# Seven-product strips: another product order, low halves last, weights traced behind the copies

## The chip, the cores and the metric

The kernel runs on one core of one Trainium2 chip. The metric is the device time in microseconds, from launch to end, as the median of a few runs. Engines are named as the profile names them: PE (TensorE matmul; PEld is its weight load, which overlaps the matmuls), DVE (VectorE), ACT (ScalarE), POOL (GpSimd) and SP (SyncE, which issues most DMAs).

## The reference

Two residual layers on a 512 x 1024 input: layer 0 mixes tokens with gated linear attention, layer 1 with softmax attention, and each is followed by a gated MLP. The change touches the MLP alone, which runs once in each layer:

```
def conv_ffn(h, w_up, w_conv, b_conv, w_down):      # h: rmsnorm(x), 512 x 1024
    u = h @ w_up                                    # 512 x 5632
    u = depthwise conv of width 3 along the tokens (u) + b_conv
    val, gate = jnp.split(u, 2, axis=-1)            # 2816 each
    return (jax.nn.silu(gate) * val) @ w_down       # 512 x 1024
x = x + conv_ffn(rmsnorm(x, norm_ffn[i]), ...)
```

All inputs and outputs are float32.

## The kernel before, in words

Every float32 product is made of three matmuls on rounded halves: a tile is split into a high half (an ACT copy to float32r) and a low half (what is left, by DVE or by an adding DMA), and high x high, high x low and low x high are summed in PSUM. Weights go the same way: a raw piece of 128 x 1024 is loaded by SP (`W.load`), ACT writes its high half `wh` (line 319 or 271) and DVE its low half `wl` (line 320), or ACT writes minus the high half (line 272) and POOL issues a DMA that adds the raw weights to it (line 308). `W.flush` issues such waiting DMAs; `W.todo` lists the pieces in the order in which they are made, and `W.ahead(n)` makes the next n.

The MLP is worked in 22 chunks of 128 gate and 128 value features, m = 0 to 21 (`ffn`, `act_up`). Chunks 0 to 5, 9, 14 and 17 are plain (`plain_up`): two feature tiles of 24 matmuls of 512 columns. The other 13 (the list `SEVEN`) are done as 2 x 2 blocks with seven products in place of eight (`seven_up`), and so are two thirds of the down projection (`down_part`, two parts of four strips, called behind chunks 9 and 17). That makes 26 + 16 such strips in both layers. Each strip is seven calls of `product`; each product is four pairs of blocks x three matmuls of 256 columns, all of them line 1074 in the profile, where the result is called `r`. So a strip is 84 matmuls.

The seven products are numbered 1 to 7. Product 1 goes to a bank of its own and ACT copies it twice (`twice`, line 1129) into the bank `both`, whose halves are r1 and r2. Product 6 adds to r2, and ACT copies r2 to the first half of a bank r3 (line 1095 in `seven_up`, 1204 in `down_part`). Product 7 goes to r4 and is copied twice to a tile `u` (or `f`). Product 4 adds to r3's first half. Product 5 adds to r2, and ACT copies r2 to r3's second half (line 1102 or 1211). `add_seven` (line 1132, DVE) adds r3 to the tile: this is one of the two results of the strip, and `act_up` then works on it (line 1117 on ACT, 1118 and 1119 on DVE). Products 2 and 3 finish the other result in `both`. Product 1 of the next strip (`begin_up`, or `begin` in `down_part`) is put between 5 and 2, to give the copies time.

The weights of a strip are four pieces (`PLACE`): piece 0 serves products 1 and 4, piece 1 serves 6 and 2, piece 2 serves 7 and 5, piece 3 serves 3. `product` asks for a piece with `W.piece`, which also makes further pieces until `PAW` = 6 (or `PA` = 4) are waiting, all of that ahead of the product's own matmuls in the traced order. PSUM has eight banks: three for `acc` (both, plain results), two for `s` (r3), two for `pt` (products 1 and 7), one other. The tiles u, f and g share three buffers.

The order of the instructions on an engine follows the order in which they are traced, but the planner that lays them out passes over an instruction that is not ready by its own estimate and takes the next that is; `tc.issue_after` pins one behind another. On the chip each engine keeps the order that was laid out.

`rescale`, called in chunk 0, scales the input and splits it by `low_dma` into `nh` and `nl`; its four adding DMAs wait in `W.pending` until the next flush. `prepare_input` later works in place on the same scaled tiles.

Of the kernel before, what the change touches and what calls it, by code (L numbers as in the profile page):

```python
# [62 lines left out]
NQ, NPART = 4, 2  # L63
# [3 lines left out]
DOWN_AFTER = {9: 0, 17: 1}  # L67


SEVEN = (6, 7, 8, 10, 11, 12, 13, 15, 16, 18, 19, 20, 21)  # L70
UPA = 3
PA = 4
# [16 lines left out]
PAW = 6  # L89
# [11 lines left out]
def hybrid_encoder_kernel(  # L101
# [23 lines left out]
    pe, act, dve, pool, sync = nc.tensor, nc.scalar, nc.vector, nc.gpsimd, nc.sync  # L125
    mm = pe.matmul
# [8 lines left out]
    def nm(s):  # L135
        uid[0] += 1
        return f"{s}{uid[0]}"
# [3 lines left out]
    def bank(tag, n):  # L141
        return pp.tile([P, S], F32, tag=tag, bufs=PS[tag], name=nm(n))
# [33 lines left out]
    class Weights:  # L176
# [127 lines left out]
        def flush(self):  # L304

            for lo, r in self.pending:
                same = lo.dtype == F32R and r.dtype != F32R
                pool.dma_start(lo.bitcast(F32) if same else lo, r, accum_op=ALU.add)
            self.pending = []

        def split(self, hi, lo, r, pieces=1, first=False):
# [28 lines left out]
    W = Weights()  # L340
# [3 lines left out]
    def add_up(layer, chunks):  # L344
        for m in chunks:
            W.add(up[layer], (m,), 4 if m in SEVEN else 2)
            if m in SEVEN and m - 1 not in SEVEN and m - 1 not in DOWN_AFTER:
                W.todo[-5:-3] = W.todo[-4], W.todo[-5]

    def add_ffn(layer):  # L350
        first = 0
        for m, part in DOWN_AFTER.items():
            add_up(layer, range(first, m + 1))
            W.add(down_w[layer], range(part * NQ, (part + 1) * NQ), 4)
            at = len(W.todo) - 4 * NQ - 1
            W.todo[at : at + 2] = W.todo[at + 1], W.todo[at]
            first = m + 1
        add_up(layer, range(first, FC))
        W.add(down_w[layer], range(NPART * NQ, down_w[layer].shape[0]))
# [135 lines left out]
    def feature_tile(*a):  # L495
        for last in feature_steps(*a):
            pass
        return last
# [518 lines left out]
    def ffn(layer, norm, cw, nxt):  # L1017
# [5 lines left out]
        down = []  # L1023
# [4 lines left out]

        def rescale():

            for p in range(KC // 2):
                xr = big(F32, "xr")
                for i in range(2):
                    c = 2 * p + i
                    dve.scalar_tensor_tensor(xr[:, i * S : (i + 1) * S], x[c], norm.weight(c), norm.R, ALU.mult, ALU.mult)
                hi, lo = big(F32R, "nh"), big(F32R, "nl")
                W.low_dma(hi, lo, xr)
                scaled.append(xr)
                fresh.extend((hi[:, i * S : (i + 1) * S], lo[:, i * S : (i + 1) * S]) for i in range(2))

        def plain_up(m):

            pss = []
            for t in range(2):
                ps = bank("s" if t else "acc", "up")
                feature_tile(*W.half(up[layer], 2 * m + t, max(UPAW if W.wide else UPA, ahead.get((m, t), 1))), norm.hl if m < SWITCH else fresh, ps)
                pss.append(ps)
                if t == 0 and m not in DOWN_AFTER:
                    begin_up(m + 1)
                if t == 0 and m in DOWN_AFTER:  # L1050
                    down.append(down_part(DOWN_AFTER[m], m))
                    next(down[-1])
# [12 lines left out]
        def product(pieces, src, strip, pairs, i, dst, start):  # L1065
            h, o = PLACE[i]
            if h not in pieces:
                pieces[h] = W.piece(src, strip, h, PAW if W.wide else PA)
            wh, wl = pieces[h]
            for j, p in enumerate(pairs):  # L1070
                sl = slice(o + j * P, o + (j + 1) * P)
                mh, ml = p[i]
                for a, (w, m) in enumerate(((wh, mh), (wh, ml), (wl, mh))):
                    mm(dst, w[:, sl], m, start=start and j == 0 and a == 0, stop=j == len(pairs) - 1 and a == 2,  # L1074
                       skip_group_check=True)
            W.flush()

        def begin_up(m):
            if m in SEVEN:
                begun.append(seven_up(m))  # L1080
                next(begun[-1])

        def seven_up(m):

            pieces = {}
            go = lambda *a: product(pieces, up[layer], m, inputs, *a)
            r = bank("pt", "r1")[:, :H]
            go(1, r, True)
            both = bank("acc", "r")
            r1, r2 = both[:, :H], both[:, H:]  # L1090
            twice(both, r)
            yield
            go(6, r2, False)
            r3 = bank("s", "r3")
            act.activation(r3[:, :H], r2, AF.Copy)  # L1095
            r4 = bank("pt", "r4")[:, :H]
            go(7, r4, True)
            d = tmp("u", "u")
            twice(d, r4)
            go(4, r3[:, :H], False)  # L1100
            go(5, r2, False)
            act.activation(r3[:, H:], r2, AF.Copy)  # L1102
            add_seven(d, r3, r4)
            yield 1, d
            begin_up(m + 1)
            go(2, r1, False)
            go(3, r2, False)
            yield 0, both

# [15 lines left out]
        H = S // 2  # L1125

        def twice(d, r4):
            two = lambda a: a.rearrange("p (o t) -> p o t", t=H)
            act.activation(two(d), two(r4).to_broadcast([P, 2, H]), AF.Copy)

        def add_seven(d, r3, r4):
            dve.tensor_tensor(d, d, r3, ALU.add)
# [49 lines left out]
        def down_part(part, m):  # L1182

            pairs = [quads.pop(part * NQ + i) for i in range(NQ)]
            st = {}
            pieces = [{} for _ in range(NQ)]
            go = lambda n, *a: product(pieces[n], w_dn, part * NQ + n, pairs, *a)

            def begin(n):
                r = bank("pt", "r1")[:, :H]
                go(n, 1, r, True)
                st[n] = bank("acc", "r")
                twice(st[n], r)

            begin(0)
            yield
            for n in range(NQ):
                r, c, d = st[n], x_home[n][:, :S], x_home[n][:, S:]  # L1200
                r1, r2 = r[:, :H], r[:, H:]
                go(n, 6, r2, False)
                r3 = bank("s", "r3")
                act.activation(r3[:, :H], r2, AF.Copy)
                r4 = bank("pt", "r4")[:, :H]
                go(n, 7, r4, True)
                g, f = tmp("u", "g"), tmp("u", "f")
                twice(f, r4)
                go(n, 4, r3[:, :H], False)
                go(n, 5, r2, False)  # L1210
                act.activation(r3[:, H:], r2, AF.Copy)  # L1211
                add_seven(f, r3, r4)
                W.pending.append((d, f))
                if n + 1 < NQ:
                    begin(n + 1)
                else:
                    begin_up(m + 1)
                go(n, 2, r1, False)
                go(n, 3, r2, False)
                act.activation(g, r, AF.Copy)  # L1220
                W.pending.append((c, g))

        def end(c, ps):
# [13 lines left out]
        for m in range(FC):  # L1237
# [15 lines left out]
            else:  # L1253
                for i, y in enumerate(held):
                    t = big(F32R, "gu")
# [343 lines left out]
```

## Time and profile before

| | |
|---|---|
| median of 3 runs | 1087.01 us (1086.85 to 1087.84) |
| profiled execution, first to last instruction | 1085.5 us |
| PE busy | 1077.5 us (99%) |
| PEld busy | 966.4 us (89%) |
| DVE busy | 888.5 us (82%) |
| ACT busy | 721.1 us (66%) |
| POOL busy | 136.7 us (13%) |
| granted TensorE clock | 1.000 |

The table is of one execution; its device time is not given apart from its span, so the 1.5 us between the span and the median of the runs stand for what lies around the span. Busy time is the share in which an engine worked on an instruction at all; weight loads and matmuls of PE overlap, and matmuls are pipelined, so the duration of one is longer than the distance between two.

### The profile page before, as it was taken

Reading aid. Unit: us, or ns where it says so; the run is one execution under the profiler, and the core shown is the slowest. Engines: PE = TensorE matmul, PEld = TensorE weight load, DVE = VectorE, ACT = ScalarE, POOL = GpSimd, SP = SyncE. Lnnn points to the kernel's source line nnn. Section 1 sums busy time; section 2 is a strip of 40 time slices with the busy share of each in tenths; the row PEclk is TensorE's granted clock in tenths of the full one; section 3 lists DMA queues with packets and bytes.
Section 4 is the critical chain, followed back from the end, with each engine's and each line's share of the span. In section 5 each row is a group of like instructions: output and inputs, shape, how many; then the busy total and the mean of one; then the engine's idle time right before and its main releaser. Section 6 shows DMA issues by size and latency. Waiting matters only on the chain.

```text
span 1085.5 us, 17391 instructions
## 1 busy us (share of the span) xinstructions
PE 1077.5 (99%) x6672; PEld 966.4 (89%) x6672; DVE 888.5 (82%) x1327; ACT 721.1 (66%) x1134; POOL 136.7 (13%) x153
## 2 busy tenths in 40 slices
PE   9999999999999999999999999999999999999998
PEld 8888988888999999999988888888889999999997
DVE  7998967569898899988755588666989889998882
ACT  8679575478775676666574677656877567666660
POOL 0212112021001100010015333002110010001000
PEclk9999999999999999999999999999999999999999
DMA  8744446499545633274767475549863473227542
GB/s 301 187 126 106 122 141 215 154 207 204 127 125 127 145 120 111 77 177 121 252 149 162 127 204 164 164 158 202 206 148 124 105 166 116 100 80 157 136 175 78
DMA packets 55763, 164.52 MB, mean 152 GB/s; under 512 B 6528, under 2 KB 7040, under 8 KB 55680
## 3 DMA queue, kind: packets, MB, share of 16 engines
q1 hardware_dynamic: 36192, 112.66, 32.2%
q0 software_dynamic: 14592, 42.21, 21.7%
q10 hardware_dynamic: 4896, 8.55, 2.1%
q8 instruction: 52, 0.85, 0.3%
q14 instruction: 31, 0.25, 0.1%
HBM read 114.89 MB, written 14.68 MB: 119 GB/s over the span
## 4 chain that ended last, share of the span: by engine, by line
PE 87%; DVE 6%; ACT 3%; DMA 2%; issue 2%; POOL 0%; SPq 0%; DVEq 0%; ACTq 0%; POOLq 0%
PE r L1074 37%; PE op L535 8%; PE vg L652 7%; PE up L482 4%; PE up L483 4%; PE up L484 4%; PE dn L483 2%; PE dn L484 2%; PE dn L482 2%; PE av L509 1%; PE A L482 1%; DVE wl L320 1%; PE A L484 1%; DMA nl<-xr 1%; PE B L484 1%
## 5 line engine op out<-in xcount | busy, mean ns | idle before, releaser
L320 DVE TENSOR_TENSOR wl<-raw,wh 128x1024 fp32r<-128x1024 f32 x156 | 189.8, 1220 | 31.3 <-ACT wh L319 31.1
L319 ACT ACTIVATE wh<-raw 128x1024 fp32r<-128x1024 f32 x156 | 162.6, 1053 | 73.4 <-PE op L535 20.7
L1074 PE MATMUL r<-gu,wh 128*128 128x256 f32 x896 | 161.2, 282 | 0.0
L1074 PE MATMUL r<-xt,wh 128*128 128x256 f32 x832 | 151.1, 283 | 0.4 <-ACT r L1095 0.3
L1074 PEld LDWEIGHTS r<-gu,wh 128*128 128x128 f32 x896 | 139.3, 190 | 1.0 <-ACT r L1211 0.2
L1074 PEld LDWEIGHTS r<-xt,wh 128*128 128x128 f32 x832 | 129.2, 190 | 1.6 <-ACT r L1095 1.1
L1074 PE MATMUL r<-gu,wl 128*128 128x256 f32 x448 | 126.3, 283 | 0.0
L1074 PE MATMUL r<-xt,wl 128*128 128x256 f32 x416 | 117.2, 283 | 0.0
L1074 PE MATMUL r<-nh,wh 128*128 128x256 f32 x312 | 88.8, 285 | 0.3 <-ACT r L1102 0.3
L1074 PE MATMUL r<-nh,wl 128*128 128x256 f32 x312 | 88.2, 283 | 0.0
L1074 PE MATMUL r<-nl,wh 128*128 128x256 f32 x312 | 87.9, 282 | 0.0
L1074 PEld LDWEIGHTS r<-gu,wl 128*128 128x128 f32 x448 | 85.1, 190 | 0.0
L1074 PEld LDWEIGHTS r<-xt,wl 128*128 128x128 f32 x416 | 79.1, 190 | 0.0
L482 PE MATMUL up<-nh,wh 128*128 128x512 f32 x192 | 75.3, 392 | 0.0
L483 PE MATMUL up<-nl,wh 128*128 128x512 f32 x192 | 75.2, 392 | 0.0
L484 PE MATMUL up<-nh,wl 128*128 128x512 f32 x192 | 75.2, 392 | 0.0
L535 PE MATMUL op<-oT,wh 128*128 128x512 f32 x256 | 72.4, 393 | 0.0
L271 ACT ACTIVATE wh<-raw 128x1024 fp32r<-128x1024 f32 x36 | 38.0, 1056 | 38.2 <-PE up L483 11.5
L1074 PEld LDWEIGHTS r<-nh,wh 128*128 128x128 f32 x312 | 59.3, 190 | 2.9 <-ACT r L1102 2.6
L1074 PEld LDWEIGHTS r<-nl,wh 128*128 128x128 f32 x312 | 59.4, 190 | 0.2
L1074 PEld LDWEIGHTS r<-nh,wl 128*128 128x128 f32 x312 | 59.4, 190 | 0.0
L535 PEld LDWEIGHTS op<-oT,wh 128*128 128x128 f32 x256 | 47.4, 188 | 9.7 <-ACT oT L937 0.3
(299 smaller groups left out, 2761.6 us busy)
## 6 DMA issues: line engine op xcount, KB each, us to landing
raw<-in_w_up_dram SPq DMA_DIRECT2D x84, 512.0 KB, 4.6
raw<-in_w_down_dram SPq DMA_DIRECT2D x44, 512.0 KB, 3.7
wl<-raw POOLq DMA_DIRECT2D x20, 512.0 KB, 5.3
wl<-in_w_up_dram POOLq DMA_DIRECT2D x16, 512.0 KB, 7.8
ring<-p ACTq DMA_DIRECT2D x32, 256.0 KB, 2.6
xw<-in_xw_dram SPq DMA_DIRECT2D x8, 512.0 KB, 6.6
raw<-in_w_v_dram SPq DMA_DIRECT2D x8, 512.0 KB, 5.9
raw<-in_w_g_dram SPq DMA_DIRECT2D x8, 512.0 KB, 4.0
```

The costliest lines, as they stand in the source:

```text
L271: act.activation(hi, r, AF.Copy)
L319: act.activation(hi[:, sl], a, AF.Copy)
L320: dve.tensor_tensor(lo[:, sl], a, hi[:, sl].bitcast(F32), ALU.subtract)
L482: mm(ps, wh, mh, start=start, stop=False)
L483: mm(ps, wh, ml, start=False, stop=False)
L484: return mm(ps, wl, mh, start=False, stop=stop)
L509: mm(ps[j][:, :width], hl[k][i == 2][:, j * P : (j + 1) * P], (wl if i == 1 else wh)[:, sl], start=k == 0 and i == 0, stop=k == KC - 1 and ...
L535: mm(pss[ng][n], wt[:, sl], mv, start=k == late[0][0] and i == 0, stop=k == late[-1][-1] and i == 2)
L652: last = mm(ps[j], m[:, js], w[:, sl], start=i in (1, 7, 2) and p == 0 and a == 0, stop=i in (4, 2, 3) and p == 3 and a == 2, skip_group_c ...
L1074: mm(dst, w[:, sl], m, start=start and j == 0 and a == 0, stop=j == len(pairs) - 1 and a == 2, skip_group_check=True)
```

## The change

Five things are altered. Within a product, the eight matmuls with high halves of weights come first and the four with low halves last. `product` takes a function `then`, the ACT copy of its result, and traces it right behind the matmuls; only behind that are further weights made (`W.ahead`), and that now happens after each product. The order of the products of a strip becomes 1; 6, 7, 2, 5, [1 of the next], 4, 3, so that products 2 and 4 have changed places, and `add_seven` comes behind product 4 and so behind product 1 of the next strip. `rescale` flushes what is pending, and then issues each of its four adding DMAs as soon as it is traced, pinned behind the last weights' DMA. A swap in `W.todo` is made only where the chunk is not one of `SEVEN`; the two chunks to which the line applies, 9 and 17, are not, so the list stays what it was. `begin` gathers the two ways in which a next strip is begun.

```
-                pool.dma_start(lo.bitcast(F32) if same else lo, r, accum_op=ALU.add)
+                self.sent = pool.dma_start(lo.bitcast(F32) if same else lo, r, accum_op=ALU.add)
...
         def rescale():
+            W.flush()
+            sent = W.sent
             for p in range(KC // 2):
...
                 W.low_dma(hi, lo, xr)
+                with tc.issue_after(sent.ins):
+                    W.flush()
...
-        def product(pieces, src, strip, pairs, i, dst, start):
+        def product(pieces, src, strip, pairs, i, dst, start, then=None):
             h, o = PLACE[i]
             if h not in pieces:
-                pieces[h] = W.piece(src, strip, h, PAW if W.wide else PA)
+                pieces[h] = W.piece(src, strip, h, 0)
             wh, wl = pieces[h]
-            for j, p in enumerate(pairs):
-                sl = slice(o + j * P, o + (j + 1) * P)
-                mh, ml = p[i]
-                for a, (w, m) in enumerate(((wh, mh), (wh, ml), (wl, mh))):
-                    mm(dst, w[:, sl], m, ...)
+            steps = [(j, wh, a) for j in range(len(pairs)) for a in range(2)]
+            steps += [(j, wl, 0) for j in range(len(pairs))]
+            for n, (j, w, a) in enumerate(steps):
+                mm(dst, w[:, o + j * P : o + (j + 1) * P], pairs[j][i][a], ...)
+            if then is not None:
+                then()
+            W.ahead((PAW if W.wide else PA) - len(W.made))
             W.flush()
...
         def seven_up(m):
...
-            go(6, r2, False)
             r3 = bank("s", "r3")
-            act.activation(r3[:, :H], r2, AF.Copy)
+            go(6, r2, False, copy(r3[:, :H], r2))
             r4 = bank("pt", "r4")[:, :H]
-            go(7, r4, True)
             d = tmp("u", "u")
-            twice(d, r4)
+            go(7, r4, True, lambda: twice(d, r4))
+            go(2, r1, False)
+            go(5, r2, False, copy(r3[:, H:], r2))
+            begin(m)
             go(4, r3[:, :H], False)
-            go(5, r2, False)
-            act.activation(r3[:, H:], r2, AF.Copy)
             add_seven(d, r3, r4)
             yield 1, d
-            begin_up(m + 1)
-            go(2, r1, False)
             go(3, r2, False)
             yield 0, both
```

`down_part` is altered in the same way: 6, 7, 2, 5, [1 of the next], 4, `add_seven`, 3, with f's adding DMA behind product 4 and g's behind product 3.

More of the change, by code (lines that the diff above doesn't have):

```diff
@@ L355, in add_ffn @@
             at = len(W.todo) - 4 * NQ - 1
-            W.todo[at : at + 2] = W.todo[at + 1], W.todo[at]
+            if m not in SEVEN:
+                W.todo[at : at + 2] = W.todo[at + 1], W.todo[at]
             first = m + 1
@@ L1047, in plain_up @@
                 pss.append(ps)
-                if t == 0 and m not in DOWN_AFTER:
-                    begin_up(m + 1)
-                if t == 0 and m in DOWN_AFTER:
-                    down.append(down_part(DOWN_AFTER[m], m))
-                    next(down[-1])
+                if t == 0:
+                    begin(m)
                 if m == 0 and t == 0:
@@ L1081, in begin_up, with begin @@
                 next(begun[-1])
+        def begin(m):
+            if m in DOWN_AFTER:
+                down.append(down_part(DOWN_AFTER[m], m))
+                next(down[-1])
+            else:
+                begin_up(m + 1)
         def seven_up(m):
@@ L1086, in seven_up @@
             go = lambda *a: product(pieces, up[layer], m, inputs, *a)
-            r = bank("pt", "r1")[:, :H]
-            go(1, r, True)
-            both = bank("acc", "r")
+            copy = lambda o, i: lambda: act.activation(o, i, AF.Copy)
+            r, both = bank("pt", "r1")[:, :H], bank("acc", "r")
             r1, r2 = both[:, :H], both[:, H:]
-            twice(both, r)
+            go(1, r, True, lambda: twice(both, r))
             yield
-            go(6, r2, False)
             r3 = bank("s", "r3")
-            act.activation(r3[:, :H], r2, AF.Copy)
+            go(6, r2, False, copy(r3[:, :H], r2))
             r4 = bank("pt", "r4")[:, :H]
-            go(7, r4, True)
             d = tmp("u", "u")
-            twice(d, r4)
+            go(7, r4, True, lambda: twice(d, r4))
+            go(2, r1, False)
+            go(5, r2, False, copy(r3[:, H:], r2))
+            begin(m)
             go(4, r3[:, :H], False)
-            go(5, r2, False)
-            act.activation(r3[:, H:], r2, AF.Copy)
             add_seven(d, r3, r4)
             yield 1, d
-            begin_up(m + 1)
-            go(2, r1, False)
             go(3, r2, False)
@@ L1189, in down_part, with first @@
             go = lambda n, *a: product(pieces[n], w_dn, part * NQ + n, pairs, *a)
-            def begin(n):
+            copy = lambda o, i: lambda: act.activation(o, i, AF.Copy)
+            def first(n):
                 r = bank("pt", "r1")[:, :H]
-                go(n, 1, r, True)
                 st[n] = bank("acc", "r")
-                twice(st[n], r)
-            begin(0)
+                go(n, 1, r, True, lambda: twice(st[n], r))
+            first(0)
             yield
@@ L1201, in down_part @@
                 r1, r2 = r[:, :H], r[:, H:]
-                go(n, 6, r2, False)
                 r3 = bank("s", "r3")
-                act.activation(r3[:, :H], r2, AF.Copy)
+                go(n, 6, r2, False, copy(r3[:, :H], r2))
                 r4 = bank("pt", "r4")[:, :H]
-                go(n, 7, r4, True)
                 g, f = tmp("u", "g"), tmp("u", "f")
-                twice(f, r4)
+                go(n, 7, r4, True, lambda: twice(f, r4))
+                go(n, 2, r1, False)
+                go(n, 5, r2, False, copy(r3[:, H:], r2))
+                if n + 1 < NQ:
+                    first(n + 1)
+                else:
+                    begin_up(m + 1)
                 go(n, 4, r3[:, :H], False)
-                go(n, 5, r2, False)
-                act.activation(r3[:, H:], r2, AF.Copy)
                 add_seven(f, r3, r4)
                 W.pending.append((d, f))
[L1214 to L1220, printed above, removed]
+                go(n, 3, r2, False, lambda: act.activation(g, r, AF.Copy))
                 W.pending.append((c, g))
```

4 lines of the change are left out of this document (2 added, 2 removed).

## The prediction

> **What bounds the kernel now.** I read the page's head first, then busy time by stretch, then the waits of the weight loads, then the queues of ACT and POOL at the places where PE waited.
>
> ```profile
> span 1085.5 us, 17391 instructions
> PE 1077.5 (99%) x6672; PEld 966.4 (89%) x6672; DVE 888.5 (82%) x1327; ACT 721.1 (66%) x1134; POOL 136.7 (13%) x153
> ```
>
> PE is idle for 8.0 us of 1085.5 (1085.5 - 1077.5). The change adds and removes no matmul, so it can act only on idle time of PE, on the distance between matmuls, or make new idle time. Next, stretches of the MLP (columns: stretch, length, busy time of each engine with the number of its instructions, clock, DMA):
>
> ```profile
> 328.00:404.00 76.00, 76.00 (x638) 75.98 (x637) 67.33 (x89) 52.48 (x82) 6.93 (x8) 1.00 0.53 132
> 419.50:445.00 25.50, 25.50 (x193) 24.33 (x192) 25.50 (x40) 17.80 (x28) 0.00 (x0) 1.00 0.32 104
> 801.00:847.00 46.00, 45.30 (x316) 41.87 (x315) 43.37 (x63) 30.75 (x48) 0.87 (x1) 1.00 0.45 129
> 847.00:923.00 76.00, 76.00 (x636) 75.82 (x636) 67.39 (x89) 52.61 (x82) 6.97 (x8) 1.00 0.54 135
> ```
>
> From 328 to 404 (four down strips, then four up strips) and in the same stage of layer 1 (847 to 923) PE is busy all the time and so are its weight loads: nothing there can be won by order. DVE is full beside it where chunks are worked on (25.50 of 25.50 from 419.5), yet PE does not wait there either. PE is short only at the start of the strips of layer 1: 45.30 of 46.00. The waits of the strips' weight loads over the whole run (us in total, times, longest):
>
> ```profile
> PEld r L1074 <- ACT r L1102: 2.6, 10, 0.5
> PEld r L1074 <- ACT r L1095: 1.1, 3, 0.7
> PEld r L1074 <- ACT r L1211: 0.2, 1, 0.2
> ```
>
> So the whole purse is 2.6 + 1.1 + 0.2 = 3.9 us in 14 waits, 0.28 us each, all for an ACT copy of a partial result and none for a weight. The rest of PE's idle time lies outside the strips, which the change does not touch.
>
> **Which of these waits the new order can take away.** The same line for L1102 in seven windows, in order: 276 to 330, 380 to 420, 420 to 460, 500 to 545, 800 to 835, 920 to 970, 980 to 1062.
>
> ```profile
> PEld r L1074 <- ACT r L1102: 0.4, 2, 0.2
> PEld r L1074 <- ACT r L1102: 0.3, 1, 0.3
> PEld r L1074 <- ACT r L1102: 0.2, 1, 0.2
> PEld r L1074 <- ACT r L1102: 0.3, 1, 0.3
> PEld r L1074 <- ACT r L1102: 0.7, 2, 0.5
> PEld r L1074 <- ACT r L1102: 0.4, 2, 0.2
> PEld r L1074 <- ACT r L1102: 0.3, 1, 0.3
> ```
>
> Eight of the ten are at the last strip of a run (chunks 8, 13, 16 and 21, twice each), where no next strip is begun between product 5 and product 2: 0.2 + 0.3 + 0.2 + 0.3 in layer 0, 0.2 + 0.4 (two) + 0.3 in layer 1, 1.9 us. Chunk 13 shows how (weight loads, then ACT):
>
> ```profile
> 403.68 0.19 PEld L1074 LDWEIGHTS r<-xt,wl 128*128 128x128 f32 x1
> 403.80 0.19 PEld L482 LDWEIGHTS up<-nh,wh 128*128 128x128 f32 x1
> 404.60 0.19 PEld L1074 LDWEIGHTS r<-nh,wh 128*128 128x128 f32 x1 [0.26 <-ACT r L1102]
> 404.18 0.37 ACT L1102 ACTIVATE r<-r 128x256 f32<-128x256 f32 x1
> ```
>
> Product 5 loads its last weights at 403.68, three matmuls of the next plain chunk are put in as filling, and product 2 (`nh`, the first after them) starts at 404.60, when the copy at 404.18 has ended. But product 2 writes r1 and the copy reads r2, another half of the same bank: the wait is by bank, not by the bytes touched. After the change product 4 stands in that place. It writes r3's first half while the same copy writes r3's second half, again one bank. So I leave these 1.9 us where they are. Elsewhere too the pairs only change names: product 2 now waits for the copy of product 6 (bank `both`) with one product between, as product 4 did (r3), and product 4 for the copy of product 5 with one product between, as product 2 did. A gain of 1.9 us would be had if writes to another half of a bank did not wait; the row excludes that for a copy that reads, and a copy that writes stands nearest to it.
>
> The Trainium skill's page "PSUM — Partial Sum Buffer", section "PSUM bank collisions raise a hardware error", says the same in general, and speaks against the swap: two engines must be kept apart by bank and quadrant, whichever addresses they touch. By that rule the eight waits stay and this part is 0; by addresses alone it would be -1.9 us. The row of chunk 13 agrees with the rule for a reading copy (0.26 us); no run here shows it yet for a writing one.
>
> That leaves 3.9 - 1.9 = 2.0 us that order could cure: two L1102 waits (0.2 and 0.5), all of L1095 (1.1), and L1211 (0.2). Most of it is one place, ACT at the start of layer 1's strips:
>
> ```profile
> 815.75 0.81 ACT L1117 ACTIVATE y<-u,cw 128x512 f32<-128x512 f32 x1 [1.18 <-DVE u L1132]
> 817.13 0.37 ACT L1095 ACTIVATE r<-r 128x256 f32<-128x256 f32 x1
> 821.12 1.04 ACT L319 ACTIVATE wh<-raw 128x1024 fp32r<-128x1024 f32 x1
> 822.07 0.36 ACT L1102 ACTIVATE r<-r 128x256 f32<-128x256 f32 x1
> 826.20 1.06 ACT L319 ACTIVATE wh<-raw 128x1024 fp32r<-128x1024 f32 x1 [1.75 <-DMA raw<-in_w_up_dram]
> 828.53 0.37 ACT L1095 ACTIVATE r<-r 128x256 f32<-128x256 f32 x1
> ```
>
> The copy at 817.13 is late because ACT stood 1.18 us on `add_seven` (L1132); the one at 822.07 stands behind the weights of 821.12; the one at 828.53 behind a weight piece whose load was 1.75 us late.
>
> **The change part by part.**
> Weights behind the copies. No instruction is added: the 1.05 us ACT copies and the DVE splits of weights move back by about one product, whose length is this:
>
> ```profile
> 279.67 1.42 PE r L1074 x12
> SPq L230 <- DVE wl L320: 335.6, 75, 18.8
> DVE xr L1168 <- DMA nl<-xr: 1.5, 1, 1.5
> ```
>
> 1.42 us, 0.118 us a matmul. This can cure the waits at 822 and 828 and the early small ones, about 0.5 + 0.7 + 0.2 + 0.2 = 1.6 us; but the hold-ups are 1.0 to 2.8 us long (a weight copy of 1.04; 1.75 + 1.06), up to twice the 1.42 us moved, so I take half, -0.8, with ends -1.6 and 0. The cost on SP's queue: loads already wait for DVE to free raw tiles (335.6 us), so they go out up to 1.42 us later. What hides that is the stock of six pieces, one and a half strips of 84 x 0.118 = 9.9 us; without it each late piece would cost up to 1.42 us.
>
> `add_seven` behind product 4.
>
> ```profile
> L1132 DVE TENSOR_TENSOR u<-u,r x26: 678/681/695, 294.7 to 1048.5; 128x512 f32<-128x512 f32 x26
> ```
>
> It becomes ready two products later (the sixth of the strip's order in place of the fourth), and what is left before the next strip's product-6 copy shrinks from products 1, 2, 3, 6 (5.7 us) to 3 and 6 (2.8 us). DVE (0.68 us for the sum) and then ACT (0.81 us, L1117) must fit in, and behind ACT's L1117 wait that copy, the other copies, and so PE. Where DVE is not full, 0.68 + 0.81 fits into 2.8 us: 0. Where it is, the wait at 815.75 is the example; I put one or two new ones at 0.28 us each: +0.4, with ends -0.3 (that one wait goes) and +5.0 (below).
>
> Low halves last. The low half is needed up to 8 x 0.118 = 0.94 us later and the high half's buffer is free three matmuls (0.35 us) earlier. No row has PE waiting for a low half, so 0 on the path. The distance of matmuls in another mix of halves is not in the trace; 1.42 us for 12 here, against 76.00 us for 638 above, is 118 and 119 ns, a band of 1 ns on 3528 matmuls (42 strips x 84), ±3.5 us at the far ends; I take 0, since both rows contain every kind of neighbour but low-low.
>
> `down_part`. f's adding DMA goes out two products later. ACT, POOL:
>
> ```profile
> 331.88 0.58 ACT L1129 ACTIVATE f<-r 128x512 f32<-128x512 f32 x1
> 338.24 0.60 ACT L1220 ACTIVATE g<-r 128x512 f32<-128x512 f32 x1 [2.30 <-PE r L1074]
> 337.32 0.87 POOL L308 DMA_DIRECT2D xd<-f  x1 [41.79 <-DVE f L1132]
> 339.13 0.87 POOL L308 DMA_DIRECT2D xd<-g  x1 [0.94 <-ACT g L1220]
> 341.96 0.58 ACT L1129 ACTIVATE f<-r 128x512 f32<-128x512 f32 x1
> DMA to landing us min/median/max: 3.7/4.0/4.3
> ```
>
> f is held from 331.88 to 337.32 + 4.0 = 341.3. Product 4 will end two products, 2.8 us, after product 5, so this DMA goes at about 340.2 and lands at 344.2, behind the next f at 341.96. Then the third of the three buffers carries it (g holds one from 338.24). ACT idles 2.30 us ahead of g, so there is slack: 0. Without a third buffer ACT would stand 2.2 us a strip. POOL's next entry, g's DMA, is at 339.13 now and so moves at most 1 us behind f's; nobody on PE waits for either.
>
> `rescale`.
>
> ```profile
> 749.86 0.87 POOL L308 DMA_DIRECT2D wl<-in_w_up_dram  x1 [5.47 <-ACT wl L272]
> 753.01 0.86 POOL L308 DMA_DIRECT2D nl<-xr  x1 [2.29 <-DVE xr L1035]
> 762.40 0.86 POOL L308 DMA_DIRECT2D nl<-xr  x1 [2.69 <-DVE y L1119]
> 770.42 0.87 POOL L308 DMA_DIRECT2D wl<-in_w_up_dram  x1 [7.15 <-ACT wl L272]
> ```
>
> The four DMAs already follow the weights' one, precede the next, and POOL waits for their data, not they for POOL: 0. Ends: the 1.5 us that DVE waits once for such a DMA (row above), won or doubled, on DVE only; PE is busy then. The `W.todo` line and `begin` are 0.
>
> **Sum.** -0.8 + 0.4 = -0.4 us: the span goes from 1085.5 to 1085.1. The median of the runs lies 1087.01 - 1085.5 = 1.5 us above the span, so 1086.6 us.
>
> **The rivals.**
> All waits go, strip ends included: 3.9 us, 1087.0 - 3.9 = 1083.1 us. For it: filling and slack are decided by small shifts, and 14 waits of 0.28 us are soon gone. Against it: the bank row. Faster by over 0.2% (2.2 us, about what this kernel's runs can tell from no change) needs more than half of the purse.
> Slower: `add_seven` late before the copy. In the strips of the stretches where DVE is full (chunks 6 to 8, 10 to 13, 15 and 16: nine a layer, 18 in all) each next product-6 copy stands behind ACT's L1117, and PE waits 0.28 us (the mean wait) once a strip, or 0.7 (the longest): 18 x 0.28 = 5.0 less the 0.8 won, 1087.0 + 4.2 = 1091.2 us. It decides from 11 strips on (11 x 0.28 - 0.8 = 2.3). For it: the 1.18 us of ACT at 815.75. Against it: from 847 to 923 the same chain runs without one wait.
> The change does nothing that can be measured: every engine keeps its work, and waits move about: 1087.0, in the same class as my forecast.
>
> **How the numbers follow.** My forecast, with no effect at all beside it, 0.58: 1085 to 1088.5. All or most waits gone, 0.21. Late `add_seven`, or another new wait of its kind, 0.21. The likeliest gives 1086.6; to leave out no more than 2 in 10 the range reaches into both rivals, 1083.9 to 1090.0. Faster 0.22, same 0.57, slower 0.21.
>
> **What would show it.** Right: in the waits, the strip-end waits remain, now by product 4 (a load `r<-xt,wh` waiting for the second copy), 1.5 to 2.3 us; the stretch 801 to 847 has less than 0.7 us of idle PE; the stretches that were full stay full. Wrong: strip-end waits gone; many waits for the first copy with ACT standing on L1132; a stretch of 76 us that grew, which would mean that the low halves' neighbourhood changed the distance of matmuls; PE waiting for `wl` or a raw load.

## The result, and the profile after

The changed kernel takes 1090.31 us (median of 5 runs, 1089.98 to 1091.22), beside 1086.85 us (1086.73 to 1087.84) for the kernel before in the same session: a ratio of 1.0032, 95% interval 1.002 to 1.0045. It is slower by 3.5 us, and lies 0.3 us above the range forecast. The profiled execution's span grew by as much, from 1085.5 to 1089.0 us. The head of its page:

```profile
span 1089.0 us, 17466 instructions
PE 1081.2 (99%) x6672; PEld 967.9 (89%) x6672; DVE 888.9 (82%) x1327; ACT 721.0 (66%) x1134; POOL 136.7 (13%) x153
```

PE has the same 6672 matmuls and is "busy" 3.7 us longer (1081.2 - 1077.5). That column hides waits: a short stand of PE lies under the modelled tail of the matmul before it. The weight loads show it. The same stretches as in the prediction, with the matching down and up strips of layer 0 (450.5 to 526) added (columns as there: stretch, length, then PE, PEld, DVE, ACT and POOL busy, clock, DMA); first before, the added stretch only, then after:

```profile
450.50:526.00 75.50, 75.50 (x634) 75.47 (x633) 67.87 (x83) 51.57 (x79) 6.94 (x8) 1.00 0.60 156
```

```profile
328.00:404.00 76.00, 75.90 (x620) 74.46 (x619) 66.14 (x84) 49.74 (x77) 6.96 (x8) 1.00 0.52 136
450.50:526.00 75.50, 75.46 (x610) 73.93 (x610) 66.77 (x82) 50.88 (x79) 6.94 (x8) 1.00 0.55 146
801.00:847.00 46.00, 46.00 (x327) 43.09 (x326) 42.15 (x61) 33.59 (x52) 1.74 (x2) 1.00 0.48 132
847.00:923.00 76.00, 75.96 (x614) 74.45 (x614) 67.64 (x84) 48.62 (x76) 6.96 (x8) 1.00 0.50 132
```

In the three steady stretches, whose loads were busy for 75.98, 75.47 and 75.82 us before (227.3 together), they are now busy for 74.46, 73.93 and 74.45 (222.8). The start of layer 1's strips, by contrast, has lost its idle time: PE is busy for 46.00 of 46.00 us, where it was 45.30. In what follows the sum of these three PEld numbers (227.3 before, 222.8 after) is the quick measure of a kernel's steady stretches.

The waits of the strips' weight loads, after (us in total, times, longest):

```profile
PEld r L1075 <- ACT r L1098: 3.3, 12, 0.7
PEld r L1075 <- ACT r L1197: 1.5, 7, 0.3
PEld r L1075 <- DMA wl<-in_w_up_dram: 0.3, 1, 0.3
```

Line 1098 is the copy after 6 or 5 in `seven_up`, 1197 the same in `down_part`. 3.9 us in 14 waits have become 5.1 in 20, and the down strips, with one wait of 0.2 us before, have seven. Each such wait also costs a little at the matmul behind the one that waited. Worked out from the starts of all matmuls of the strips: gaps of more than 140 ns between neighbours held 2.72 us above the normal 120 ns before, 5.86 us after. The difference, 3.1 us, is nearly the whole loss. The normal gap itself did not move: below 140 ns the gaps fall short of 120 ns by 2.10 us in all before, and by 2.03 after.

**How one such wait comes about.** The same strip in both kernels, DVE and then ACT, before (start, duration, line, operation; in brackets the idle time ahead and what ended it):

```profile
348.22 0.69 DVE L286 TENSOR_TENSOR wl<-raw,wh 128x512 fp32r<-128x512 f32 x1 [2.25 <-PE r L1074]
348.83 1.22 DVE L293 TENSOR_TENSOR sum<-raw,raw 128x1024 f32<-128x1024 f32 x1
349.77 0.37 ACT L1204 ACTIVATE r<-r 128x256 f32<-128x256 f32 x1 [0.90 <-PE r L1074]
350.08 1.06 ACT L319 ACTIVATE wh<-sum 128x1024 fp32r<-128x1024 f32 x1
351.05 1.04 ACT L319 ACTIVATE wh<-raw 128x1024 fp32r<-128x1024 f32 x1
```

and after:

```profile
349.02 0.69 DVE L286 TENSOR_TENSOR wl<-raw,wh 128x512 fp32r<-128x512 f32 x1 [0.27 <-PE r L1075]
349.62 1.22 DVE L293 TENSOR_TENSOR sum<-raw,raw 128x1024 f32<-128x1024 f32 x1
350.88 1.06 ACT L319 ACTIVATE wh<-sum 128x1024 fp32r<-128x1024 f32 x1 [0.85 <-DVE sum L293]
351.85 1.04 ACT L319 ACTIVATE wh<-raw 128x1024 fp32r<-128x1024 f32 x1
352.79 0.37 ACT L1197 ACTIVATE r<-r 128x256 f32<-128x256 f32 x1
353.21 0.89 PEld L1075 LDWEIGHTS r<-gu,wh 128*128 128x128 f32 x7 [0.21 <-ACT r L1197]
```

Piece 3 of a strip, the one that product 3 alone uses, has its halves in a ring of three small buffers (`summed`, h = 3), so the next strip's low half (DVE, line 286) has to wait until product 3 has read one of its two halves for the last time. Behind line 286 the code pins the sum of line 293 (`tc.issue_after(self.last.ins)`), and behind the sum ACT makes two high halves (line 319). Product 6 comes right after product 3, and its copy goes to ACT too. So two chains race for ACT, and both start at the end of product 3:

- the weights: from the start of line 286 to the end of line 293, 350.05 - 348.22 = 1.83 us before, 350.84 - 349.02 = 1.82 after;
- the copy after 6: from the start of line 286, 349.77 - 348.22 = 1.55 us before.

Before, the copy has a lead of 0.28 us. With the low halves last, the high half is read for the last time by the 8th matmul of product 3 and no longer by the 11th, so line 286 starts three matmuls earlier, 3 x 0.12 = 0.36 us, against the copy. The lead is gone, and the planner, which orders by its own estimate, puts two weight copies ahead: the copy after 6 starts 352.79 - 349.02 = 3.77 us behind line 286. Product 2 waits for it. In the laid-out order eight matmuls of the next product 1 stand as filling ahead of product 2, but they are then missing as cover between product 5 and product 4, and product 4 waits as well (0.25 us at 356.85). Over the run, the copy stands 3.77 us behind line 286 in seven strips (two weight copies ahead) and 2.83 in four (one ahead), ten of these eleven in the three steady stretches; before, it never stands more than 1.62 us behind there.

### The profile page after: what moved, and what is told of

It reads as the page before. It is cut to its first block, busy times and chain, and to the rows that moved or that the text cites. A ratio compares the mean times of both kernels' runs of the same rounds, so it can differ in the third digit from the quotient of the medians.

```text
span 1089.0 us, 17466 instructions
## 1 busy us (share of the span) xinstructions
PE 1081.2 (99%) x6672; PEld 967.9 (89%) x6672; DVE 888.9 (82%) x1327; ACT 721.0 (66%) x1134; POOL 136.7 (13%) x153
## 4 chain that ended last, share of the span: by engine, by line
PE 85%; DVE 7%; issue 3%; DMA 2%; ACT 2%; POOL 0%; SPq 0%; DVEq 0%; ACTq 0%; POOLq 0%
PE r L1075 35%; PE op L536 8%; PE vg L653 7%; PE up L483 4%; PE up L484 4%; PE up L485 4%; PE dn L485 2%; PE dn L484 2%; PE dn L483 2%; DVE wl L320 1%; PE av L510 1%; PE A L483 1%; PE A L485 1%; PE B L485 1%; PE A L484 1%
## 5 line engine op out<-in xcount | busy, mean ns | idle before, releaser
L1075 PE MATMUL r<-gu,wh 128*128 128x256 f32 x896 | 127.0, 284 | 0.1
L1075 PEld LDWEIGHTS r<-gu,wh 128*128 128x128 f32 x896 | 115.6, 190 | 3.0 <-ACT r L1197 1.5
L1075 PE MATMUL r<-xt,wh 128*128 128x256 f32 x832 | 117.2, 283 | 0.5 <-ACT r L1098 0.3
L1075 PEld LDWEIGHTS r<-xt,wh 128*128 128x128 f32 x832 | 107.0, 190 | 3.2 <-ACT r L1098 2.6
L1075 PE MATMUL r<-gu,wl 128*128 128x256 f32 x448 | 71.5, 283 | 0.0
L1075 PE MATMUL r<-xt,wl 128*128 128x256 f32 x416 | 66.9, 283 | 0.0
L1075 PEld LDWEIGHTS r<-gu,wl 128*128 128x128 f32 x448 | 61.4, 191 | 0.0
L1075 PEld LDWEIGHTS r<-xt,wl 128*128 128x128 f32 x416 | 57.2, 191 | 0.0
L320 DVE TENSOR_TENSOR wl<-sum,wh 128x1024 fp32r<-128x1024 f32 x42 | 51.2, 1219 | 4.6 <-ACT wh L319 4.4
L319 ACT ACTIVATE wh<-sum 128x1024 fp32r<-128x1024 f32 x42 | 44.3, 1055 | 12.8 <-DVE sum L293 12.4
```

Of the source, the lines that this page charges most:

```text
L319: act.activation(hi[:, sl], a, AF.Copy)
L320: dve.tensor_tensor(lo[:, sl], a, hi[:, sl].bitcast(F32), ALU.subtract)
L1075: mm(dst, w[:, o + j * P : o + (j + 1) * P], pairs[j][i][a], start=start and n == 0, stop=n == len(steps) - 1, skip_group_check=True)
```

## The experiments

Theory A: product 3's high half comes free too early, and weight copies get ahead of the copy after 6. Rivals: B, the order of the products or the banks; C, the weights that are traced behind the copies, or the DMAs. The diffs are shortened; in them `mixed` stands for the order of before, high, high, low for each pair of blocks. Each ratio is to the kernel before on the same chip. Beside the experiments the kernel before had medians of 1087.1 to 1087.5 us, and single runs from 1086.2 to 1089.6, so rows are best compared by their ratios. The last column is the sum of PEld over the three steady stretches, from profiled executions (a_pinned has none, since its work is shifted against the stretches by 5 us and more).

| kernel | what it is | us | ratio (95%) | PEld, us |
|---|---|---|---|---|
| before | | 1086.85 | 1 | 227.3 |
| after | | 1090.31 | 1.0032 (1.002 to 1.0045) | 222.8 |
| a_mixed_in_3 | after, product 3 mixed | 1087.48 | 1.0002 (0.9993 to 1.0011) | 226.3 |
| a_high_at_end | after, a high matmul last in 3 | 1087.39 | 1.0 (0.9991 to 1.0009) | 226.1 |
| a_high_3_before_end | after, the 8th high matmul 9th in 3 | 1087.91 | 1.0004 (0.9995 to 1.0013) | 226.0 |
| b_low_last_in_3 | before, low last in 3 | 1089.64 | 1.0019 (1.001 to 1.0027) | 224.3 |
| b_low_last | before, low last in all | 1089.48 | 1.0018 (1.001 to 1.0027) | 223.6 |
| b_low_last_in_124567 | before, low last in all but 3 | 1087.29 | 0.9998 (0.9989 to 1.0006) | 226.5 |
| b_low_last_in_567 | before, low last in 5, 6, 7 | 1086.53 | 0.9996 (0.9987 to 1.0004) | 227.2 |
| a_old_order | after, old order of products | 1089.15 | 1.0013 (1.0004 to 1.0022) | 224.4 |
| a_old_rest | after, without the two other parts | 1090.66 | 1.003 (1.0019 to 1.0042) | 223.0 |
| a_mixed_halves | after, all mixed | 1090.02 | 1.0022 (1.0013 to 1.0031) | 224.5 |
| a_low_last_in_5_only | after, all mixed but 5 | 1089.39 | 1.0017 (1.0008 to 1.0026) | 226.0 |
| a_low_last_in_1_5 | after, all mixed but 1 and 5 | 1088.18 | 1.0007 (0.9998 to 1.0016) | 226.3 |
| a_pinned | after, weights made behind 6 and 7 only | 1107.42 | 1.018 (1.0166 to 1.0194) | |

**Product 3 alone, out of after and into before.** One line undoes the halves' order in after for product 3; the other kernel is before with that order in product 3 alone.

```
 steps = [(j, wh, a) for j in range(len(pairs)) for a in range(2)]
 steps += [(j, wl, 0) for j in range(len(pairs))]
+if i == 3: steps = mixed         # a_mixed_in_3
+if i != 3: steps = mixed         # b_low_last_in_3, in before
```

> The changed kernel, with the halves of product 3 alone mixed as before (high, high, low for each pair); the other six products keep their low halves last. Theory A (early release): product 3's low halves last free its high half three matmuls (0.36 us) sooner, so DVE's low half of the next piece 3 (L286) and the sum behind it (L293) start sooner, two ACT weight copies get ahead of the copy after product 6, and PE waits for that copy. Then this one edit takes the loss back: 1086.3 to 1087.5 us, waits of the down strips' weight loads for the copies (1.5 us in 7) near 0. Rival B (order): products 2 and 4 having changed places makes the waits, by bank; then nothing changes, 1089.5 to 1091. Rival C (weights traced later): also 1089.5 to 1091.

> The kernel before, with the low halves last in product 3 alone and nothing else changed. Theory A: the loss appears, 1 to 3.5 us, 1088 to 1090.5 us, with L319 weight copies ahead of the copy after product 6 in the first down strips and PE waiting for L1204 or L1095. Rivals B and C: no difference, 1086.5 to 1087.3 us.

Both came out as A said. The order within one product of seven takes the loss away from after (1087.48) and brings the larger part of it into before (1089.64; 0.0019 of 0.0032). In the steady stretches two weight copies stand ahead of the copy after 6 in eight strips of b_low_last_in_3 and in none of a_mixed_in_3. The ACT queue of b_low_last_in_3 at the same strip has after's order:

```profile
350.18 1.06 ACT L319 ACTIVATE wh<-sum 128x1024 fp32r<-128x1024 f32 x1 [0.78 <-DVE sum L293]
351.14 1.04 ACT L319 ACTIVATE wh<-raw 128x1024 fp32r<-128x1024 f32 x1
352.09 0.36 ACT L1205 ACTIVATE r<-r 128x256 f32<-128x256 f32 x1
```

**Is it the release of the buffer, or the place of the low halves?** Two kernels leave the low halves late and move only the last reading of the high half in product 3.

```
+if i == 3: steps = steps[:7] + steps[8:] + steps[7:8]                  # a_high_at_end
+if i == 3: steps = steps[:7] + steps[8:9] + steps[7:8] + steps[9:]     # a_high_3_before_end
```

> After, product 3 alone in another order: seven matmuls with the high half, the four with the low half, then the eighth with the high half. The low halves are still late, but the buffer of the high half comes free with the product's last matmul, as in the kernel before. Theory A (the loss is the early release of product 3's high half, which lets two weight copies go on ACT ahead of the copy after product 6): the loss goes, 1086.5 to 1088.3 us, as with the halves of product 3 mixed (1087.48). Rival B (the neighbourhood or lateness of the low halves costs something by itself): it stays at 1089.5 to 1090.5 us.

> After, product 3 alone with its eighth high-half matmul behind the first low one, so that the high half's buffer comes free three matmuls ahead of the product's end instead of four (0.36 us instead of 0.48). Theory A as a race with a tipping point: two weight copies get ahead of the copy after 6 only when the buffer is free early enough; at three matmuls they do not, and the loss goes nearly whole: 1086.5 to 1088.0 us, steady stretches as with the eighth at the very end (1087.39). Rival (the loss grows with each matmul by which the buffer comes free earlier, 2.9 us over four): 1089.0 to 1090.0 us.

It is the release. With one high-half matmul at the end the loss is gone (1087.39), and with it just one matmul later than in after the loss is gone too (1087.91). It does not grow with the earliness; it tips between the ninth and the eighth matmul. The queues of a_high_3_before_end, DVE and then ACT, show how narrowly:

```profile
348.92 0.69 DVE L286 TENSOR_TENSOR wl<-raw,wh 128x512 fp32r<-128x512 f32 x1 [0.39 <-PE r L1077]
349.53 1.22 DVE L293 TENSOR_TENSOR sum<-raw,raw 128x1024 f32<-128x1024 f32 x1
350.71 0.37 ACT L1199 ACTIVATE r<-r 128x256 f32<-128x256 f32 x1 [0.90 <-PE r L1077]
350.99 1.05 ACT L319 ACTIVATE wh<-sum 128x1024 fp32r<-128x1024 f32 x1
```

There the copy starts 1.79 us behind line 286, and the sum is ready 1.83 us behind it: the copy still wins, by 0.04 us. In a_high_at_end the same two starts are:

```profile
348.65 0.69 DVE L286 TENSOR_TENSOR wl<-raw,wh 128x512 fp32r<-128x512 f32 x1 [0.63 <-PE r L1077]
350.20 0.37 ACT L1199 ACTIVATE r<-r 128x256 f32<-128x256 f32 x1 [0.90 <-PE r L1077]
```

The distances fit a count of matmuls from the first release of one of product 3's two halves to the end of product 6: 13 after the 11th matmul (before 1.55 us, and a_high_at_end 350.20 - 348.65 = 1.55, where the 11th reads the low half for the last time, so that a buffer comes free there and not, as its expectation has it, at the 12th), 15 after the 9th (1.79), 16 after the 8th (1.89 in those strips of after where the copy still goes first); 13, 15 and 16 x 0.119 are 1.55, 1.79 and 1.90. Against 1.83 for the sum only the last can lose. It does not lose everywhere: in three strips of after's steady stretches the copy goes first at 1.89 us. The order on ACT is the one that the planner laid out by its own estimate, and that estimate is in no trace; so the runs show between which matmuls the order tips, and the measured distances only stand near the planner's.

**The other products in the old order.**

```
+if i not in (1, 2, 4, 5, 6, 7): steps = mixed    # b_low_last_in_124567, in before
+if i not in (5, 6, 7): steps = mixed             # b_low_last_in_567, in before
```

> Before with the low halves last in all seven products, nothing else. Theory A: as with product 3 alone (1089.64), 1088.8 to 1090.0 us; the order of products, the weights traced behind the copies and the DMAs behind the weights' ones add less than 1 us to after's 1090.31. Rival C (half of the loss or more lies in those other parts, and low halves last in the products beside 3 win something): 1087.0 to 1088.3 us.

> Before with the low halves last in every product but 3. Theory A: what hurts is product 3 alone, so nothing is lost: 1086.0 to 1087.8 us. Rival (low halves last cost wherever they are): 1088.5 to 1090 us, as with them in all seven (1089.48).

> Before with the low halves last in products 5, 6 and 7 alone: a candidate for a faster kernel, since the high halves that come free early there lie ahead of no urgent copy. Theory A: 1086.0 to 1087.3 us, within 0.1% of before; faster than 1086 only if some of the 3.9 us of waits for copies go.

Low halves last in all seven cost what they cost in product 3 alone (1089.48 and 1089.64), and in the six others nothing (1087.29). The candidate with 5, 6 and 7 has a median of 1086.53 us and an interval that includes 1: its waits for copies are 2.9 us on the weight loads, 1.0 less than before, all of it in a few places, and that is at the edge of what can be told. No kernel here is shown to be faster than before.

**The other parts of the change.**

```
# a_old_order: the calls of products 2 and 4 change back, begin behind 5, add_seven ahead of it
# a_old_rest:
-pieces[h] = W.piece(src, strip, h, 0)
+pieces[h] = W.piece(src, strip, h, PAW if W.wide else PA)
-W.ahead((PAW if W.wide else PA) - len(W.made))     # behind `then`
-W.flush(); sent = W.sent                           # in rescale, and the pinned flushes
```

> The changed kernel with the products in the order of before (6, 7, 4, 5, [1 of the next], 2, 3, and add_seven behind 5); low halves last and weights behind the copies stay. Theory A: still slow, 1088.5 to 1090.5 us, since product 3 stays last and its high half is freed early. Rival B (order): back to 1086.5 to 1087.5. Rival C: 1089.5 to 1091.

> After without the two other parts: weights made at the start of a product as before, and the normalised input's DMAs traced as before; the order of products and the low halves last stay. Theory A (neither part matters): 1089.5 to 1091.0 us. Rival C (the weights traced behind the copies are what lets PE wait): 1087 to 1088.5 us.

The weights behind the copies and the DMAs of `rescale` are worth nothing that can be told (1090.66 without them, 1090.31 with). The old order of products leaves a loss (1089.15, an interval clear of 1), so the loss does not need the new order; the new order may add to it, but the intervals of the two overlap.

**A miss: mixing all seven.** If product 3 is the place, mixing everywhere should cure it as well.

```
-steps = high halves, then low halves
+steps = mixed                              # a_mixed_halves
+if i != 5: steps = mixed                   # a_low_last_in_5_only
+if i not in (1, 5): steps = mixed          # a_low_last_in_1_5
```

> The changed kernel with the halves mixed as before in all seven products. Theory A: the same as with product 3 alone mixed, 1086.3 to 1087.5 us, within 0.7 us of it. If low halves last cost something in the other six products too, this one is faster than that by more. Rivals B and C: 1089.5 to 1091.

It did not: 1090.02 us. In the steady stretches of its trace no weight copy stands ahead of the copy after 6, so product 3 is cured; PE stands elsewhere. So the new order is not free either: with the halves mixed it costs 0.0022 of the time (with the two other parts in it, which are worth nothing that can be told), about as much as low halves last cost in the kernel before (b_low_last, 0.0018). Both together, in after, cost 0.0032. One row is a wait for a DMA at the third matmul of a product 1, which in the mixed order is the first low one (PE):

```profile
301.36 0.39 PE L1074 MATMUL r<-nh,wl 128*128 128x256 f32 x1 [0.96 <-DMA wl<-in_w_up_dram]
```

and the first matmuls of product 4 stand in 19 strips, 1.8 us in all. Product 4 waits for the copy after 5, so product 5 was set back first:

> After, halves mixed in six products, low halves last in product 5 alone. Mixed in all seven it ran at 1090.02, in product 3 alone at 1087.48. Theory A with a second place: a weight copy that is released by the last matmul of product 5 (mixed) stands ahead of the copy after 5 for its whole 1.06 us, and the 12 matmuls of product 1 (1.43 us) no longer cover weight and copy; low halves last in 5 free it 0.5 us earlier, so the copy after 5 follows in time, and product 4's waits (19 first matmuls, 1.8 us, with halves mixed everywhere) shrink: 1086.5 to 1088.3 us. Rival (it is another product's mixing, or the 1.1 us wait for one wl DMA alone): 1089 to 1090.5 us.

> After, halves mixed in five products, low halves last in products 1 and 5. With product 5 alone it ran at 1089.39 and PE stood 0.95 us once, at the third matmul of a product 1, for the DMA that brings its wl; with the low halves last that matmul is the ninth, 0.7 us later. Theory A completed (mixing costs in the new order at two places, the copy after 5 and this DMA): the DMA wait shrinks to 0.3 us or less, 1087.3 to 1088.7 us. Rival (the wait for wl is only one sign of something else): 1089 to 1090 us.

The first missed: 1089.39. Its steady stretches did come back (PEld 226.0, from 224.5), so product 5 is a second place where the order of halves counts; but the wait for that wl stayed, and a wait of the attention part for a ring buffer was 1.4 us where a_mixed_in_3 has 0.7 (weight loads of both):

```profile
PEld pt L1457 <- DMA ring<-p: 1.4, 1, 1.4
PEld r L1077 <- DMA wl<-in_w_up_dram: 1.0, 1, 1.0
```

With product 1's low halves last as well, its first low matmul is the ninth, 0.7 us later; the wl wait is gone and the time is 1088.18. So in the new order the low halves last win something in products 5 and 1, and lose in 3. Weight copies stand ahead of the copy after 5 in both kernels, but with 5 mixed they start later (ACT, a_mixed_halves and then a_low_last_in_5_only):

```profile
478.97 1.06 ACT L319 ACTIVATE wh<-raw 128x1024 fp32r<-128x1024 f32 x1 [1.28 <-PE r L1074]
480.46 0.36 ACT L1196 ACTIVATE r<-r 128x256 f32<-128x256 f32 x1
```

```profile
477.32 1.06 ACT L319 ACTIVATE wh<-raw 128x1024 fp32r<-128x1024 f32 x1 [0.93 <-PE r L1077]
478.81 0.36 ACT L1199 ACTIVATE r<-r 128x256 f32<-128x256 f32 x1
```

The copy after 6 starts at 474.87 and 473.58 there, so the weight copy, which PE releases, starts 4.10 us behind it with 5 mixed and 3.74 without, and the copy after 5 follows 5.59 and 5.23 us behind. Four strips of a_mixed_halves have 5.59 there (from 474.87, 495.21, 871.15 and 891.55); the same strips of a_low_last_in_5_only have 5.23 twice and 5.11 twice. So here an earlier release helps, since the weight goes first in both. That this is the whole difference was not tested.

**A miss: the weights pinned.** A direct cure, meant to leave the buffers as in after and to keep weight copies from going ahead of the copy after 6:

```
+done = then() if then is not None else None
+if i in (6, 7):
+    with tc.issue_after(done.ins):
         W.ahead((PAW if W.wide else PA) - len(W.made))
```

> After, with its order of products and halves, but weights are made ahead only after products 6 and 7, and there pinned behind that product's copy. Nothing is freed at another time; what changes is that no weight copy can stand ahead of the copy after 6. Theory A: the waits for the copy after 6 go, 1086.0 to 1088.0 us, unless weights made at fewer places come late (then waits of PE for wh or wl, and the time says little). Rival B (the loss is in the order of the products or in the banks): 1089.5 to 1091 us with the same waits for copies.

It took 1107.42 us and says little on A, as its expectation allowed for: weights made at two places of seven come late. In the eleven strips where weights went ahead in after, the copy after 6 now goes first (1.91 us behind line 286 at 354.53, say), though in others, as behind 470.54, two weights still stand ahead of it; the strips' loads wait for copies for 3.8 us in 17 waits, where after has 4.8 in 19. The waits of PE (the same wait is listed for the loads too):

```profile
PE r L1075 <- DMA wl<-in_w_up_dram: 7.3, 2, 3.7
PE up L485 <- DMA wl<-in_w_up_dram: 3.7, 1, 3.7
```

These are 11 of the 17 us by which it is slower than after. Pinning without starving the weights was not tried.

## Why the prediction was wrong

- **Low halves last: "0 on the path". This is the step that failed.** It named the earlier release ("the high half's buffer is free three matmuls (0.35 us) earlier") and asked only whether PE waits for a low half and whether the gap between matmuls changes. Both answers hold: no steady stretch waits for a low half, and the gap is the same. What it did not ask is what the earlier release sets off. The chain was in the trace of before: line 286 released by PE, line 293, line 319, and the copy after 6 with a lead of 0.28 us. In product 3 the term measures +2.9 us (after against a_high_at_end: 1090.31 and 1087.39; 3.5 by their ratios), where 0 was taken; in the kernel before, low halves last in all seven cost 0.0018 of the time, 2.0 us. Taken out of all seven products of after it gives back next to nothing (1090.02), since in the new order low halves last win about as much in other products, 5 and 1 among them, as they lose in 3; the prediction had neither.
- **"Nothing there can be won by order", and "the stretches that were full stay full".** They could be lost. 227.3 us of busy loads became 222.8. "The pairs only change names" took for granted that the copies come as early as before; in eleven strips one or two weight copies, 0.94 us each (2.83 - 1.89), now go ahead of them. And the change of names is not free by itself: with the halves mixed as before, the new order runs at 1.0022 of the time before, with product 4's first matmul late in 19 strips.
- **Weights behind the copies, -0.8.** Measured with the `rescale` part: 1090.66 without, 1090.31 with, nothing that can be told. Tracing them later does not make the planner place them later where it finds ACT free. The gain at the start of layer 1's strips came (45.30 to 46.00 of 46.00), but it is there with the old order and low halves last in 3 alone too, 45.97:

```profile
801.00:847.00 46.00, 45.97 (x323) 42.69 (x322) 42.88 (x62) 32.56 (x51) 1.74 (x2) 1.00 0.45 128
```

- **`add_seven` behind product 4, +0.4, and the rival built on it (1091.2).** The rival's time was near, its mechanism was not. Before the copy at 817.13 ACT had stood 1.18 us for `add_seven`; in after the same wait is 0.42 us and the copy of the strip is already done (ACT):

```profile
820.31 0.37 ACT L1098 ACTIVATE r<-r 128x256 f32<-128x256 f32 x1 [2.07 <-PE r L1075]
821.09 0.82 ACT L1124 ACTIVATE y<-u,cw 128x512 f32<-128x512 f32 x1 [0.42 <-DVE u L1139]
```

- **Strip ends: the waits stay.** Right: 2.0 us in six waits, where 1.9 in eight were and 1.5 to 2.3 were forecast. At the end of chunk 13 product 4 now waits for the copy that writes the other half of its bank, longer than product 2 did (0.69 against 0.26 us), since ACT was at line 1124 when product 5 ended (weight load, then ACT):

```profile
408.06 0.66 PEld L1075 LDWEIGHTS r<-xt,wh 128*128 128x128 f32 x5 [0.69 <-ACT r L1098]
407.64 0.36 ACT L1098 ACTIVATE r<-r 128x256 f32<-128x256 f32 x1
```

  By the Trainium skill's page "PSUM — Partial Sum Buffer", section "PSUM bank collisions raise a hardware error", the two must be kept apart; this row agrees with it for a copy that writes, which the prediction had left open: the program waits. No run here shows what would happen without the wait.
- **`down_part` and `rescale`, 0.** Right as far as it can be seen: f's DMA now goes 1.28 us ahead of g's (349.04 and 350.32 on POOL), nobody on PE waits for either, and a_old_rest shows nothing for `rescale`.

## What to carry to other kernels

An operand that is released earlier is not only a gain: look up in the trace what the release starts, follow that chain to the next engine that it shares with the urgent work, and compare the two arrival times. Here a lead of 0.28 us was lost to an advance of 0.36 us, and a kernel whose PE looked full had nothing to take up 1 to 2 us of delay. Where PE is busy all the time by the modelled ends, read the busy time of its weight loads; and when one part of a change hurts, undo it in one place only, since the same edit may help in another.

## What the runs showed of the hardware

In a_pinned PE stood 3.64 us for one DMA, and behind that the matmuls came at less than their normal pace for 5.4 us. The stretches before the wait, in it, behind it and later (columns as above):

```profile
280.00:292.00 12.00, 12.00 (x81) 11.04 (x80) 6.67 (x12) 5.75 (x9) 0.87 (x1) 1.00 0.15 45
292.90:296.60 3.70, 0.17 (x2) 0.00 (x0) 3.70 (x7) 3.70 (x6) 0.00 (x0) 0.81 0.68 128
296.70:302.10 5.40, 5.40 (x25) 5.40 (x26) 0.41 (x1) 2.24 (x5) 0.87 (x1) 0.51 0.77 187
302.10:314.00 11.90, 11.86 (x97) 11.47 (x96) 10.77 (x14) 6.49 (x10) 0.00 (x0) 1.00 0.44 135
```

25 matmuls in 5.40 us are 216 ns each, where 120 is normal, at a granted clock of 0.51. So this stand of 3.6 us cost 25 x 0.096 = 2.4 us more behind it. That is not a fixed price: behind the stand of 3.70 us that ended at 829.62, ten matmuls came at about 120 ns first, and the slow stretch was shorter (columns as above):

```profile
829.70:831.00 1.30, 1.30 (x11) 1.30 (x12) 0.27 (x1) 1.29 (x4) 0.87 (x1) 1.00 0.69 176
831.10:834.40 3.30, 3.30 (x17) 3.30 (x17) 0.00 (x0) 0.61 (x2) 0.00 (x0) 0.50 0.87 192
```

The waits for copies, 0.7 us at the longest, show no such thing: the clock is 1.00 in all their stretches. They cost some 0.10 us at the second matmul instead: of the 22 matmuls that waited first in products 2 and 4 of after (3.3 us), the next one was late too, as were a few more (27 in all, 2.7 us).
